# GLU stage of a streaming encoder on one Trainium2 core: operand stores moved to GpSimd's queue in two groups per tile, a third yT slot, meta frames split early, and state products later in the SSM

## The chip, the core and the metric

The kernel runs on one core of a Trainium2 chip, in one launch. The metric is the time of one execution on the device, in microseconds; the time of a kernel is the median of its runs. The core's engines each work through their own instructions in the order in which they were written: TensorE (PE, with PEld for its weight loads), VectorE (DVE), ScalarE (ACT), GpSimd (POOL) and SyncE (SP), which does nothing but issue DMAs here. DMAs can be issued from SP, from ACT and from POOL; each issue waits in its engine's queue for what it needs, and holds up whatever stands behind it.

## What is computed

One layer of a hybrid encoder on 2048 frames of 1024 numbers, with 16 learned meta frames ahead of them. Cut to what matters:

```python
hn = rms_norm(h, norm_mix)
u  = hn @ w_in                         # 64 groups of 16 channels
s_t = a * s_{t-1} + B u_t              # diagonal complex state, 64 per group
y  = gelu(Re(C s) + d_skip * u)
a, g = split(y @ w_glu)                # 1024 x 2048
h  = h + a * sigmoid(g)                # the GLU stage ends here
hn = rms_norm(h, norm_ffn)
b  = causal_dwconv(hn @ w_up)          # 1024 x 5632, three taps
b1, b2 = split(b)
out = h + (silu(b1) * b2) @ w_down     # 2816 x 1024
```

All of it is float32 in and out. Large products are taken as three float16 products of high and low halves (hi x hi, hi x lo, lo x hi).

## The kernel before

The program has three stages.

**The SSM stage.** The channels go in eight blocks of 128 (`cb`, 0 to 7). For each block, `emit_y` forms the outputs. Frames stand as 128 chunks of 16; for each pair of groups (`gp`, 0 to 3) a PSUM tile `yp` (tag `y`, two slots, which the small meta tile `mp` also uses) collects *direct* products, of the block's inputs `U` with a Toeplitz matrix (L588), and *carried* products, of the chunk states `Z` with `CA` (L590). ACT then takes the gelu of the whole tile (L592). `Toep` comes back from DRAM by eight DMAs, and right behind them on SP come the four DMAs that bring the states from `S` into `Z`. In this kernel direct and carried products alternate within one `gp`: one direct product of group 0, then its carried product, and so on. `mid`, when given, does a piece of the splitting of `w_glu` after each gelu.

**The GLU stage.** Sixteen tiles of 128 frames, `t` = 0 to 15 (`tile_of_step` gives the frames). For each tile: `load_y` brings `y` from DRAM (SP), `prep_y` splits it into `yT` (hi on ACT, L126; lo on DVE, L129; two slots), `glu_mm` does 96 matmuls of 512 columns on PE (L138) into four PSUM banks, alternately one of two sets of four, and `glu_post` does the rest: two sigmoids on ACT (L935), two products and two sums on DVE (L936, L937), the store of `h` (SP), the sum of squares on ACT (L940), the reciprocal root on POOL (L70, L72), the normalised tile `hn` on DVE (L943), and the splits into `hl` by `split2` (cast on ACT, L919; difference on DVE, L920). Odd tiles add and subtract halves of `hn` (L962, L963, L973, L974) and make three casts. SP then transposes `hl` into `hc` (L957) and stores part of it in `hd` (L982). The order of the instructions is written out by hand: what a function issues takes its place in each engine's queue at that point of the program.

Into this loop `keep_down` is woven. It is a generator that prepares the 77 operands of the down projection for the next stage: for each of 11 pairs of row blocks of `w_down` it loads two 512 KB pieces on POOL (`dst`, L874), makes seven operands, five of which are a sum or a difference formed on POOL (L889) and two of which are taken as they are, and for each operand casts the high half on ACT (L891), yields, takes the low half on DVE (L893), and stores the 256 KB result in DRAM one step late through `pend` (L896, SP). The results stand in four slots `wk`, one after the other (`NA = 4`). `keep(n)` takes n steps. Steps are taken at the head of the loop, between `prep_y` and `glu_post`, inside `glu_post` and behind it: six per tile.

The 16 meta frames pass the GLU in small products: `meta_load` brings `ytm` in after tile 3's load, `glu_meta` (at t = 3) splits it into `ym` (L995, L996) and issues 256 tiny matmuls (L1000, L1003) ahead of `glu_post(3)`, and `glu_meta2` (at t = 4) normalises.

**The FFN stage.** It streams the operands of the up and down projections through PE twice (`kb` = 0, 1). Its first weights are loaded by `w_load`, which is called at t = 14 behind `glu_post(14)`, and cast by `w_units` at t = 15 ahead of `glu_post(15)`.

Of the kernel before, what the change touches and what calls it, by code (L numbers as in the profile page):

```python
# [10 lines left out]
F16 = mybir.dt.float16  # L11
F32 = mybir.dt.float32
# [3 lines left out]
P = 128  # L16
D = 1024
DK = 8
# [26 lines left out]
def tile_kernel(ctx: ExitStack, tc: tile.TileContext, x, meta, norm_mix, norm_ffn, w_in, lam_re, lam_im, log_dt,  # L45
# [57 lines left out]
            A.copy(wg[0][:, dk, cs_], st)  # L103
            PO.tensor_tensor(wg[1][:, dk, cs_], st, wg[0][:, dk, cs_], op=ALU.subtract)

    yts = {}

    def tile_of_step(n):
        return n // 2 + 8 * (n % 2)
# [8 lines left out]
    def prep_y(t, d0=0, d1=DK, eng=A):  # L118

        w = P * (d1 - d0)  # L120
        if t not in yT:
            yT[t] = gl.tile([P, 2, DK, P], F16, tag="yT", bufs=2, name=f"yT_{t}")
        yt = yts.pop(t)
        hi, lo = (yT[t][:, i, d0:d1].rearrange("p b k -> p (b k)") for i in range(2))
        if eng is A:
            A.activation(hi, yt[:, 0:w], AF.Copy, scale=YS)  # L126
        else:
            V.tensor_scalar(hi, yt[:, 0:w], YS, None, op0=ALU.mult)
        V.scalar_tensor_tensor(lo, yt[:, 0:w], YS, hi, op0=ALU.mult, op1=ALU.subtract)  # L129
# [12 lines left out]
    with ExitStack() as c2:  # L142
# [424 lines left out]
        def emit_y(cb, mid=None):  # L567
            u, tp, ca, z = U[cb], Toep[cb], CA[cb], Z[cb]

            mp = psum.tile([P, 2], F32, tag="y", name=f"mp{cb}")  # L570
            for b in range(2):
                for f in range(2):
                    c0 = 224 if f == 0 else 96
                    for i in range(4):
                        g = 4 * b + i
                        PE.matmul(out=mp[32 * i:32 * i + 32, b:b + 1], lhsT=tp[:, g, c0:c0 + 32],
                                  rhs=u[:, 1 - f, g, 0:1], start=(f == 0), stop=(f == 1))
            mf = s5.tile([P, 2], F32, tag="mf", name=f"mf{cb}")
            A.activation(mf, mp, AF.Gelu_apprx_tanh)
            A.dma_start(out=ymd[:, :, cb], in_=mf)  # L580
            yf = s5.tile([P, 2, G, P], F32, tag="yf", name=f"yf{cb}")
            for gp in range(4):
                yp = psum.tile([P, 2, 2, P], F32, tag="y", name=f"yp{cb}_{gp}")
                for i in range(2):
                    g = 2 * gp + i
                    for r in range(2):
                        for f in range(r + 1):
                            PE.matmul(out=yp[:, r, i], lhsT=tp[:, g, P * (r - f):P * (r - f) + P],  # L588
                                      rhs=u[:, 1 - f, g, 1:P + 1], start=f == 0, stop=False)
                        PE.matmul(out=yp[:, r, i], lhsT=ca[:, g, 8 * r + 1:8 * r + 9].rearrange("p a b -> p (a b)"),  # L590
                                  rhs=z[:, g], start=False, stop=True)
                A.activation(yf[:, :, 2 * gp:2 * gp + 2], yp, AF.Gelu_apprx_tanh)  # L592
                if mid:
                    mid(gp)
            PO.dma_start(out=yd[cb].rearrange("r p g k -> p r g k"), in_=yf)

        def drive(*gens):
# [266 lines left out]
    def keep_down():  # L864

        lo_, hi_ = slice(0, 512), slice(512, 1024)
        st, n = {}, itertools.count()

        def load(j):
            if j < NH:  # L870
                for r in range(2):
                    st[j, r] = fw.tile([P, D], F32, tag="wst", bufs=NW, name=f"dst{j}_{r}")
                    f = j + NH * r
                    PO.dma_start(out=st[j, r], in_=w_down[0, f * P:(f + 1) * P])  # L874

        load(0)
        pend = None
        for j in range(NH):
            load(j + 1)
            s0, s1 = st.pop((j, 0)), st.pop((j, 1))  # L880
            b11, b12, b21, b22 = s0[:, lo_], s0[:, hi_], s1[:, lo_], s1[:, hi_]
            ta, tb = (fw.tile([P, 512], F32, tag="wtmp", bufs=1, name=f"dtmp{j}_{i}") for i in range(2))
            steps = [((1, j, 1), b11, None), ((0, j, 1), b22, None),
                     ((1, j, 0), ta, (b21, b11, ALU.subtract)), ((2, j, 0), b21, (b21, b22, ALU.add)),
                     ((0, j, 0), tb, (b12, b22, ALU.subtract)), ((2, j, 1), b22, (b11, b22, ALU.add)),
                     ((3, j, 0), b12, (b11, b12, ALU.add))]
            for (s, j_, i), src, sm in steps:
                if sm:
                    PO.tensor_tensor(src, sm[0], sm[1], op=sm[2])  # L889
                w = fw.tile([P, 2, 512], F16, tag=f"wc{next(n) % NA}", bufs=1, name=f"wk{s}_{j_}_{i}")  # L890
                A.activation(w[:, 0], src, AF.Copy, scale=GS)  # L891
                yield
                V.scalar_tensor_tensor(w[:, 1], src, GS, w[:, 0], op0=ALU.mult, op1=ALU.subtract)  # L893
                if pend:
                    pend()
                pend = (lambda w=w, k=kept["d", s, j_, i]: SY.dma_start(out=wcd[k], in_=w))  # L896
        pend()
        yield

# [6 lines left out]

    with ExitStack() as c3:
        gp = c3.enter_context(tc.tile_pool(name="gp", bufs=2, side="right"))
        x2 = {}

        def load_x2(t):
# [8 lines left out]
            V.tensor_tensor(dst[:, 1], src, dst[:, 0], op=ALU.subtract)  # L920

        kd_ = keep_down()

        def keep(n):
            for _ in range(n):
                next(kd_, None)

        def glu_post(t):
# [7 lines left out]
                V.scalar_tensor_tensor(sg[:, cs_], pt[o], 1.0 / (GS * YS), sg[:, cs_], op0=ALU.mult, op1=ALU.mult)  # L936
                V.tensor_tensor(h1[:, cs_], sg[:, cs_], h1[:, cs_], op=ALU.add)  # L937
            SY.dma_start(out=h1d[tile_of_step(t)], in_=h1)
            keep(1)
            A.activation(sg, h1, AF.Square, accum_out=ss)  # L940
            rs = rstd_of(gp, ss, P, f"b{t}")
            hn = hns[t] = gp.tile([P, D], F32, tag="hn", name=f"hn{t}")
            V.scalar_tensor_tensor(hn, h1, rs, gfr, op0=ALU.mult, op1=ALU.mult)  # L943
            keep(1)
            n = 20 if odd else 8
            hl = gp.tile([P, 2, n, P], F16, tag=f"hl{odd}", bufs=1, name=f"hl{t}")
            hf = hl.rearrange("p a n c -> p a (n c)")
# [11 lines left out]
            if odd:  # L959
# [3 lines left out]
                V.tensor_tensor(hn[:, lo_], hp[:, lo_], hn[:, lo_], op=ALU.subtract)  # L963
                split2(hf[:, :, 512:1536], hn)
                turn(12, 20)
                keep(1)
                if t == T - 1:
                    w_units(5)
                split2(hf[:, :, 0:512], sg[:, lo_])
# [7 lines left out]
            else:  # L977
                split2(hf, hn)
                turn(0, 8)
                keep(1)  # L980
            for i in range(2):
                SY.dma_start(out=hd[i][j, :, P * b0:P * (b0 + n)], in_=hf[64:128, i])  # L982

# [2 lines left out]
        def meta_load():  # L986
            for tt in range(2):
                SY.dma_start(out=ytm[:, tt], in_=ymd.rearrange("(i t h) b c -> t h b i c", t=2, h=16)[tt])
            SY.dma_start(out=xm, in_=meta[14:16].rearrange("t (c p) -> (t c) p", p=P))

        def glu_meta():

            ym = gp.tile([P, DK, 2, 2], F16, tag="ym", bufs=1, name="ym")
            ytr = ytm.rearrange("p t c -> p c t")
            A.activation(ym[:, :, 0], ytr, AF.Copy, scale=YS)  # L995
            V.scalar_tensor_tensor(ym[:, :, 1], ytr, YS, ym[:, :, 0], op0=ALU.mult, op1=ALU.subtract)  # L996
            pm = psum.tile([P, 16, 4], F32, tag="u", name="gm")
            for o in range(16):
                for dk in range(DK):
# [50 lines left out]
        prep_y(2)  # L1050
        load_y(3, gp_tile)
        meta_load()
        glu_post(0)
        for t in range(1, T):
            keep(1)
            if t + 1 < T:
                load_x2(t + 1)
            if t + 2 < T:
                prep_y(t + 2)
                if t + 3 < T:  # L1060
                    load_y(t + 3, gp_tile)
            keep(1)
            if t == 4:
                glu_meta2(*ms)
            if t == 3:
                ms = glu_meta()
            if t == T - 1:
                cl.close()
                ring[0] = fl = ctx.enter_context(tc.tile_pool(name="fl", bufs=2))
                w_units(3)  # L1070
                w_chain(0, 0)
            glu_post(t)
            keep(1)
            if t + 1 < T:
                glu_mm(t + 1)
            if t == T - 2:
# [316 lines left out]
```

## Time and profile before

| | us |
|---|---|
| median of 3 runs | 2102.34 |
| the runs | 2102.34, 2109.95, 2099.18 |
| the profiled execution's own time | 2114.33 |
| its span | 2112.5 |
| mean granted TensorE clock | 0.959 |
| PE busy | 1919.9 (91%) |
| DVE busy | 1531.7 (73%) |
| ACT busy | 643.3 (30%) |
| POOL busy | 707.0 (33%) |

All times in a profile count from the start of its span. The profiled execution took 12 us more than the median; its own time is 1.8 us more than its span. In a row of a timeline stand the start, the length, the engine, the line of the kernel, the operation, what it writes and reads, and in brackets how long the engine sat idle before it and what ended that. A matmul of 512 columns is shown with about 380 ns, though they start about 216 ns apart at the full clock, since they overlap. In the views of waits, each row has a total in us, a count, and the longest.

### The profile page before, as it was taken

The numbers are of one execution on the slowest core, as the hardware profiler recorded it, in microseconds if no ns is written. First come the engines' busy times: TensorE is split into PE (matmuls) and PEld (weight loads), VectorE is DVE, ScalarE is ACT, GpSimd is POOL, SyncE is SP. The second block draws the span as 40 slices with busy tenths as digits, with TensorE's granted clock in tenths as the row PEclk, the third lists the DMA queues.
The fourth block names the chain that finished last, engine by engine and source line by source line (L and its number), as shares of the span: only waits on it lengthen the run. The fifth ranks groups of instructions, "written<-read, shape, count | busy, mean of one in ns | idle before, by whom it ended". The sixth has DMA issues, their size and how long they took to land.

```text
span 2112.5 us, 29565 instructions
## 1 busy us (share of the span) xinstructions
PE 1919.9 (91%) x11116; PEld 965.2 (46%) x11116; DVE 1531.7 (73%) x2084; ACT 643.3 (30%) x1083; POOL 707.0 (33%) x749
## 2 busy tenths in 40 slices
PE   3797999679599888899999999899999999999999
PEld 3455665644344333344444444344444444444444
DVE  4489988955556555699999999895266666668882
ACT  4432322403323323354444443111022223232110
POOL 4221211413233332454556666661000001216730
PEclk9898999889799999999999999999999999999999
DMA  9957557884476666744543436954533333336443
GB/s 197 194 113 147 123 129 143 191 218 132 143 194 204 176 192 162 218 144 151 162 153 130 150 130 178 205 151 119 155 100 104 101 102 103 100 104 156 130 123 96
DMA packets 315626, 312.90 MB, mean 148 GB/s; under 512 B 116556, under 2 KB 220188, under 8 KB 315484
## 3 DMA queue, kind: packets, MB, share of 16 engines
q1 hardware_dynamic: 294396, 257.43, 46.5%
q0 software_dynamic: 11664, 38.84, 6.7%
q10 hardware_dynamic: 9424, 14.76, 2.8%
q8 instruction: 87, 1.43, 0.3%
q14 instruction: 55, 0.45, 0.1%
HBM read 180.93 MB, written 102.69 MB: 134 GB/s over the span
## 4 chain that ended last, share of the span: by engine, by line
PE 52%; DVE 18%; DMA 11%; issue 7%; ACT 4%; SPq 3%; POOL 2%; DVEq 0%; ACTq 0%; POOLq 0%
PE p L76 10%; PE p L78 10%; PE p L77 10%; PE po L76 5%; PE po L77 5%; PE po L78 5%; DMA wcd<-wk 4%; DMA fst<-in_ffn_w_up_dram 2%; PE g L138 1%; DMA Z<-S 1%; PE yp L588 1%; DVE wk L893 1%; DMA hnT<-hl 1%; PE yp L590 1%; DVE x L937 1%
## 5 line engine op out<-in xcount | busy, mean ns | idle before, releaser
L76 PE MATMUL p<-hc,wc 128*128 128x512 f16 x1232 | 468.8, 380 | 6.9 <-ACT wc L852 3.6
L78 PE MATMUL p<-hc,wc 128*128 128x512 f16 x1232 | 469.0, 381 | 6.5 <-DVE wc L858 6.3
L77 PE MATMUL p<-hc,wc 128*128 128x512 f16 x1232 | 468.6, 380 | 0.9 <-DMA hc<-hl 0.9
L138 PE MATMUL g<-wg,yT 128*128 128x512 f16 x1536 | 344.7, 387 | 27.7 <-DVE sg L936 27.7
L138 PEld LDWEIGHTS <-yT 128*128 128x128 f16 x1536 | 152.5, 99 | 218.0 <-issue 45.0
L76 PE MATMUL po<-wc,act 128*128 128x512 f16 x616 | 236.8, 384 | 12.1 <-DVE res L1343 8.3
L77 PE MATMUL po<-wc,act 128*128 128x512 f16 x616 | 236.6, 384 | 0.0
L78 PE MATMUL po<-wc,act 128*128 128x512 f16 x616 | 236.5, 384 | 0.0
L78 PEld LDWEIGHTS <-wc 128*128 128x128 f16 x1232 | 120.8, 98 | 156.1 <-DVE wc L858 8.9
L76 PEld LDWEIGHTS <-wc 128*128 128x128 f16 x1232 | 120.7, 98 | 145.6 <-issue 5.4
L77 PEld LDWEIGHTS <-wc 128*128 128x128 f16 x1232 | 120.8, 98 | 138.9 <-issue 2.5
L858 DVE SCALAR_TENSOR_TENSOR wc<-fst,wc 128x512 f16<-128x512 f32 x132 | 126.1, 959 | 23.1 <-ACT t8b L1184 11.1
L76 PE MATMUL u<-hnT,win 128*128 128x512 f16 (+2 forms) x352 | 114.1, 335 | 31.4 <-DMA hnT<-hl 29.0
L1239 ACT CAST act<-hc 128x512 f16<-128x512 f32 x88 | 54.1, 618 | 255.3 <-DVE hc L1238 149.5
L77 PE MATMUL u<-hnT,win 128*128 128x512 f16 (+2 forms) x352 | 113.9, 334 | 9.4 <-DMA hnT<-hl 9.4
L852 ACT ACTIVATE wc<-fst 128x512 f16<-128x512 f32 x132 | 79.4, 625 | 128.6 <-POOL fst L832 118.8
L1236 POOL TENSOR_TENSOR hc<-act 128x512 f32<-128x512 f16 x66 | 93.0, 1415 | 75.4 <-DVE hc L1238 75.4
L1343 DVE SCALAR_TENSOR_TENSOR res<-po,res 128x512 f32<-128x512 f32 x96 | 60.7, 682 | 77.1 <-PE po L78 76.3
L1191 POOL COPY hu<-halo 128x2 f32<-128x2 f32 x44 | 12.1, 283 | 311.5 <-DVE act L1124 191.1
L78 PE MATMUL u<-hnT,win 128*128 128x512 f16 (+2 forms) x352 | 113.9, 334 | 0.0
L1115 ACT ACTIVATE act<-hu,cwt 128x1024 f32<-128x1024 f32 x44 | 54.6, 1241 | 182.3 <-DVE hu L1207 133.4
L1240 DVE TENSOR_TENSOR act<-hc,act 128x512 f16<-128x512 f32 x88 | 95.4, 1104 | 16.8 <-ACT act L1239 14.1
(370 smaller groups left out, 3249.5 us busy)
## 6 DMA issues: line engine op xcount, KB each, us to landing
wc<-wcd SPq DMA_DIRECT2D x308, 256.0 KB, 2.7
wcd<-wc SPq DMA_DIRECT2D x154, 256.0 KB, 2.0
fst<-in_ffn_w_up_dram SPq DMA_DIRECT2D x44, 512.0 KB, 5.4
wcd<-wk SPq DMA_DIRECT2D x77, 256.0 KB, 3.4
dst<-in_ffn_w_down_dram POOLq DMA_DIRECT2D x22, 512.0 KB, 5.4
ud<-us SPq DMA_DIRECT2D x32, 258.0 KB, 4.6
U<-ud SPq DMA_DIRECT2D x16, 516.0 KB, 6.1
Toep<-kd SPq DMA_DIRECT2D x64, 128.0 KB, 5.5
```

What stands on the lines that cost most here:

```text
L76: PE.matmul(out=ps, lhsT=sh, rhs=mh, start=first, stop=False)
L77: PE.matmul(out=ps, lhsT=sh, rhs=ml, start=False, stop=False)
L78: PE.matmul(out=ps, lhsT=sl, rhs=mh, start=False, stop=last)
L138: PE.matmul(out=gps[t][o], lhsT=yT[t][:, a, dk], rhs=wg[b][:, dk, 512 * o:512 * o + 512], start=(dk == 0 and a + b == 0), stop=(dk == DK - ...
L588: PE.matmul(out=yp[:, r, i], lhsT=tp[:, g, P * (r - f):P * (r - f) + P], rhs=u[:, 1 - f, g, 1:P + 1], start=f == 0, stop=False)
L852: A.activation(w[:, 0], src, AF.Copy, scale=GS)
L858: V.scalar_tensor_tensor(w[:, 1], src, GS, w[:, 0], op0=ALU.mult, op1=ALU.subtract)
L1115: A.activation(y, hu[:, 2:18], AF.Identity, bias=cwt[:, 3, c:c + 1], scale=cwt[:, 2, c:c + 1])
L1236: PO.tensor_tensor(t_, act16[:, fa_, ra, 1], act16[:, fb, rb, 1], op=op)
L1239: A.copy(act16[:, fd, rd, 0], s_)
L1240: mix_los.append(lambda: V.tensor_tensor(act16[:, fd, rd, 1], s_, act16[:, fd, rd, 0], op=ALU.subtract))
L1343: V.scalar_tensor_tensor(h, po[t4, i], sign / (GS * AS), h, op0=ALU.mult, op1=ALU.add)
```

## The change

In the SSM's `emit_y`, the products of a `gp` are taken apart into `direct(gp)` and `carried(gp)`, and the direct products of the next `gp` are issued ahead of the carried products of this one. Only the first product of a PSUM tile carries the start flag. In the GLU stage, `yT` gets three slots (the third in another pool), all tiles' tags changed accordingly. `keep_down` gets a yield behind its first load, and that first step is taken before the loop; its stores are issued by POOL instead of SP; its steps are taken in two groups of three, at the head of the loop and behind `glu_post`, and none inside `glu_post`. The split of the meta frames moves from `glu_meta` into `meta_prep`, called right behind `meta_load`.

```diff
-    yts = {}
+    yts, yt_pools = {}, [gl, gl]
...
-            yT[t] = gl.tile([P, 2, DK, P], F16, tag="yT", bufs=2, name=f"yT_{t}")
+            yT[t] = yt_pools[t % 3].tile([P, 2, DK, P], F16, tag=f"yT{t % 3}", bufs=1, name=f"yT_{t}")
...
-            for gp in range(4):
-                yp = psum.tile([P, 2, 2, P], F32, tag="y", name=f"yp{cb}_{gp}")
+            yps = {}
+
+            def direct(gp):
+                yp = yps[gp] = psum.tile([P, 2, 2, P], F32, tag="y", name=f"yp{cb}_{gp}")
                 for i in range(2):
                     g = 2 * gp + i
                     for r in range(2):
                         for f in range(r + 1):
                             PE.matmul(out=yp[:, r, i], lhsT=tp[:, g, P * (r - f):P * (r - f) + P],
-                                      rhs=u[:, 1 - f, g, 1:P + 1], start=f == 0, stop=False)
+                                      rhs=u[:, 1 - f, g, 1:P + 1], start=i + r + f == 0, stop=False)
+
+            def carried(gp):
+                yp = yps.pop(gp)
+                for i in range(2):
+                    g = 2 * gp + i
+                    for r in range(2):
                         PE.matmul(out=yp[:, r, i], lhsT=ca[:, g, 8 * r + 1:8 * r + 9].rearrange("p a b -> p (a b)"),
-                                  rhs=z[:, g], start=False, stop=True)
+                                  rhs=z[:, g], start=False, stop=i + r == 2)
                 A.activation(yf[:, :, 2 * gp:2 * gp + 2], yp, AF.Gelu_apprx_tanh)
                 if mid:
                     mid(gp)
+
+            direct(0)
+            for gp in range(4):
+                if gp < 3:
+                    direct(gp + 1)
+                carried(gp)
...
         load(0)
+        yield
         pend = None
...
-                pend = (lambda w=w, k=kept["d", s, j_, i]: SY.dma_start(out=wcd[k], in_=w))
+                pend = (lambda w=w, k=kept["d", s, j_, i]: PO.dma_start(out=wcd[k], in_=w))
...
+        yt_pools.append(gp)
...
         kd_ = keep_down()
+        next(kd_)
...
             SY.dma_start(out=h1d[tile_of_step(t)], in_=h1)
-            keep(1)
             A.activation(sg, h1, AF.Square, accum_out=ss)
             rs = rstd_of(gp, ss, P, f"b{t}")
             hn = hns[t] = gp.tile([P, D], F32, tag="hn", name=f"hn{t}")
             V.scalar_tensor_tensor(hn, h1, rs, gfr, op0=ALU.mult, op1=ALU.mult)
-            keep(1)
...
                 turn(12, 20)
-                keep(1)
...
                 turn(0, 8)
-                keep(1)
...
-        def glu_meta():
+        def meta_prep():
 
             ym = gp.tile([P, DK, 2, 2], F16, tag="ym", bufs=1, name="ym")
...
+            return ym
+
+        def glu_meta(ym):
...
         meta_load()
+        ym = meta_prep()
         glu_post(0)
         for t in range(1, T):
-            keep(1)
+            keep(3)
...
-            keep(1)
             if t == 4:
                 glu_meta2(*ms)
             if t == 3:
-                ms = glu_meta()
+                ms = glu_meta(ym)
...
             glu_post(t)
-            keep(1)
+            keep(3)
```

## The prediction

> **What bounds the kernel now.** I read the page first (shares of the engines, the granted clock over the span), then the span cut at the stages' borders, then in the GLU stage who waits for whom, and last the instructions of each engine in order of time.
>
> ```profile
> span 2112.5 us, 29565 instructions
> PE 1919.9 (91%) x11116; PEld 965.2 (46%) x11116; DVE 1531.7 (73%) x2084; ACT 643.3 (30%) x1083; POOL 707.0 (33%) x749
> PEclk9898999889799999999999999999999999999999
> ...
> 160.00:452.00 292.00, 238.40 (x2152) 173.70 (x2151) 257.25 (x518) 83.16 (x157) 61.33 (x83) 0.89 0.73 151
> 484.00:855.00 371.00, 312.62 (x1615) 141.93 (x1613) 211.01 (x235) 118.89 (x187) 113.46 (x118) 0.92 0.64 178
> 855.00:2112.50 1257.50, 1229.27 (x6247) 562.59 (x6246) 960.23 (x1086) 374.12 (x623) 471.95 (x454) 0.99 0.47 135
> ```
>
> Columns of the last three: stretch, its length, busy time (count) of PE, PEld, DVE, ACT and POOL, granted clock, DMA share, GB/s. PE holds 91% of the whole, but the stage that changes is not PE's: from 484 to 855 us it is busy 313 of 371 us, at a clock of 0.92, and no other engine is fuller. The FFN behind it is PE's and keeps its length; what the change is worth lies ahead of 855 us. The waits from 484 to 851:
>
> ```profile
> ACT wk L891 <- DMA wcd<-wk: 114.1, 19, 15.1
> PE g L138 <- DVE sg L936: 27.7, 11, 7.6
> PE gm L1000 <- DVE ym L996: 23.9, 1, 23.9
> ...
> L896 SPq DMA_DIRECT2D wcd<-wk x77: 319/609/9194, 497.8 to 827.1; - x77
> DMA to landing us min/median/max: 2.0/3.4/15.0
> ```
>
> ACT stands 114 us before a cast of a kept operand, because the store that frees its slot has not landed, though a store lands in 3.4 us once issued. PE's 27.7 us are a consequence: it waits for banks that `glu_post` has yet to read. Why the stores come late is seen in tile 7, an odd one:
>
> ```profile
> 687.86 4.46 SPq L957 DMA_TRANSPOSE hc<-hl  x2
> 692.37 2.26 SPq L982 DMA_DIRECT2D hd<-hl  x2
> 694.67 1.09 SPq L896 DMA_DIRECT2D wcd<-wk  x1
> ...
> 699.90 0.63 ACT L891 ACTIVATE wk<-dtmp 128x512 f16<-128x512 f32 x1 [10.06 <-DMA wcd<-wk]
> ```
>
> The store stands on SP behind transposes that wait for the tile's last cast; it goes out at 694.67, lands near 699.8, and ACT, which has the next sigmoid right behind that cast, sat 10.06 us. So the stage is a chain through ACT's queue, and its measure is the start of each tile's first sigmoid, S(t):
>
> ```profile
> 485.92 1.08 ACT L935 ACTIVATE sg<-g 128x512 f32<-128x512 f32 x2
> ...
> 600.78 1.07 ACT L935 ACTIVATE sg<-g 128x512 f32<-128x512 f32 x2
> ...
> 805.63 1.07 ACT L935 ACTIVATE sg<-g 128x512 f32<-128x512 f32 x2
> 822.59 1.06 ACT L935 ACTIVATE sg<-g 128x512 f32<-128x512 f32 x2
> 836.33 1.08 ACT L935 ACTIVATE sg<-g 128x512 f32<-128x512 f32 x2
> ```
>
> These are S(0), S(4), S(12), S(13) and S(14): 114.9 us for the first four tiles, 204.9 for the next eight (51.2 a pair), 30.7 for the last two. PE needs 96 x 0.216 = 20.7 us for a tile, 41.5 a pair, so it is not the bound. Behind S(14) the loads of the FFN's first weights follow at a fixed distance, so the FFN starts as S(14) does.
>
> **The change, part by part.** *A tile's own work, without steps in it.* From tile 8 (S = 700.43) and tile 13 (S = 822.59, whose steps were nearly over):
>
> ```profile
> 705.93 2.28 DVE L943 SCALAR_TENSOR_TENSOR hn<-x,rsb,gfr 128x1024 f32<-128x1024 f32 x1 [1.54 <-POOL rsb L72]
> 709.32 1.22 DVE L920 TENSOR_TENSOR hl<-hn,hl 128x1024 f16<-128x1024 f32 x1 [0.51 <-ACT hl L919]
> 705.87 1.25 POOL L889 TENSOR_TENSOR dst<-dst 128x512 f32<-128x512 f32 x1
> ...
> 828.27 1.28 DVE L943 SCALAR_TENSOR_TENSOR hn<-x,rsb,gfr 128x1024 f32<-128x1024 f32 x1 [1.55 <-POOL rsb L72]
> 836.46 1.23 DVE L920 TENSOR_TENSOR hl<-hn,hl 128x1024 f16<-128x1024 f32 x1 [1.11 <-ACT hl L919]
> ```
>
> An even tile's last DVE instruction ends 710.5 - 700.4 = 10.1 us behind its S, an odd one's 837.7 - 822.6 = 15.1, or 16.1 with `hn` at 2.28 instead of 1.28 us. Those 2.28 us show the second thing to count: `hn` began 0.06 us behind a POOL sum of 1.25 us and was held for most of it. DVE and POOL shut each other out; a step's DVE half is 0.68 us alone and about 1.75 beside a POOL sum.
>
> The Trainium skill, "SBUF — State Buffer", section "Who interferes with whom", states this as a rule: a VectorE instruction with two SBUF inputs and a GpSimd instruction that reads SBUF exclude each other. The trace agrees (2.28 against 1.28). It goes on that DMAs issued from GpSimd starve beside VectorE's two-port modes, and advises the hardware queues. I see no such mode in this loop's steady work, so the sum by it is the same.
>
> *The steps, in two groups, stores on POOL.* SP loses 77 issues x 0.61 = 47 us, which costs nothing and gains only order: `h1d`, transposes, `hd` and `yt` no longer have stores among them. POOL gains 77 issues. No 256 KB store from POOL is in the trace; the nearest rows:
>
> ```profile
> yd<-yf POOLq DMA_DIRECT2D x8, 1024.0 KB, 4.5
> dst<-in_ffn_w_down_dram POOLq DMA_DIRECT2D x22, 512.0 KB, 5.4
> wcd<-wc SPq DMA_DIRECT2D x154, 256.0 KB, 2.0
> ...
> L874 POOL DMA_DIRECT2D dst<-in_ffn_w_down_dram x22: 527/536/625, 460.0 to 766.4; - x22
> ```
>
> Issue: 0.55 us. Landing: from 2.0 (same size, from SP, in the FFN) to 5.4 (twice the size, a load on POOL); I take SP's own 3.4, nearest in size, direction and stage. On POOL a step is a store (0.55) and, in five of seven, a sum (1.27): 1.85 us. Queued behind a store that waits: the next sum, `x2`'s load, and this tile's reciprocal root, so now the tile's own chain passes POOL. The store of step k needs DVE's half of k, which needs ACT's half, which needs the sum of k; with DVE held by the next sum every second step takes 2.5 instead of 1.85, a mean of 2.2. Then an even tile, all steps with sums: DVE free at 10.1, half of the waiting step 10.8, store and sum 12.6, four more steps at 2.2 give 21.4, the cast 0.63 and `prep_y` 1.04 give S(t+1) at 23.0. Six steps hold 4.3 sums, not 6, and 1.7 loads of 0.55. A step without a sum is not free: a cast needs the store of four steps back, issued two steps back, so two steps take at least 0.55 + 3.4 = 4.0 us. Laying the seven-step cycle against the groups position by position, an even tile comes to 20.9 to 23.5; I take 21.8, and for an odd one 6.0 more, 27.8. That is 49.6 a pair against 51.2. The waits for SP go, and what is late next is the string store, sum, cast, half; the steps also lose the cover they had inside `glu_post`.
>
> *Third yT slot, early ym.* `prep_y(2)` need not wait for `glu_mm(0)`: PE ends tile 0 after 144 of the 156 matmuls of
>
> ```profile
> 452.27 33.83 PE L138 MATMUL g<-wg,yT 128*128 128x512 f16 x156
> 483.55 1.06 ACT L126 ACTIVATE yT<-yt 128x1024 f16<-128x1024 f32 x1 [22.87 <-PE g L138]
> 553.47 0.20 ACT L995 ACTIVATE ym<-ytm 128x16 f16<-128x16 f32 x1
> 561.54 1.06 ACT L935 ACTIVATE sg<-g 128x512 f32<-128x512 f32 x2
> 586.93 0.17 DVE L1023 MEMSET one<- 128x128 f32 x1
> 589.85 0.17 DVE L1030 TENSOR_TENSOR hm<-hm,gains 128x16 f32<-128x16 f32 x1
> ```
>
> at 452.27 + 144 x 0.216 = 483.4, so S(0) is there instead of at 485.92: 2.5 gained. `ym` is now split long before PE wants it, so PE's 23.9 us at tile 3 go, and with them the 7 us that ACT stood for the tiny products (553.5 to 561.5). Of this only ACT's part counts, as PE is not the bound. What stays is about 1 us at t = 3 and 3 us (586.9 to 590.0) at t = 4. S(0) to S(1) has one group: even tile to the last cast 8, three steps 4.5, `prep_y` 1: 13.5. The early `load(0)` costs two POOL issues, 1.1 us, while POOL waits for DVE anyway: nothing; without that cover, 1.1.
>
> *The sum in the GLU stage.* S(0) to S(4): 13.5 + 27.8 + 21.8 + 27.8 + 4 = 94.9, against 114.9: 20.0 gained. S(4) to S(12): 4 x 49.6 = 198.4, against 204.9: 6.5 gained. S(12) to S(14): 21.8, then tile 13 with its last two operands and no `prep_y`: 16.1 + 0.7 + 0.55 + 1.27 + 0.63 = 19.3; together 41.1 against 30.7: 10.4 lost, since three steps were taken in tile 0 before and now stand behind tile 13. With S(0): 2.5 + 20.0 + 6.5 - 10.4 = 18.6 gained.
>
> *The SSM's products.* From block 1 of `emit_y`, and the waits for the states:
>
> ```profile
> PE yp L590 <- DMA Z<-S: 18.9, 8, 10.1
> 207.67 0.77 PE L590 MATMUL yp<-Z,CA 128*128 128x128 f32 x2 [1.01 <-DMA Z<-S]
> 214.63 0.39 PE L590 MATMUL yp<-Z,CA 128*128 128x128 f32 x2
> 217.29 0.60 ACT L592 ACTIVATE yf<-yp 128x512 f32<-128x512 f32 x1 [1.64 <-PE yp L590]
> 219.52 0.60 ACT L592 ACTIVATE yf<-yp 128x512 f32<-128x512 f32 x1 [1.64 <-PE yp L590]
> ```
>
> A `gp` is ten products in 2.23 us, 0.223 each. One direct product stood ahead of the wait, now twelve: 11 x 0.223 = 2.45 us that can fill it. But the wait is (18.9 - 10.1) / 7 = 1.26 us in seven blocks and long only in the last: filled 7 x 1.26 + 2.45 = 11.3. Against that stands a new wait: `direct(2)` takes the slot of `yp0` right behind `carried(0)`, so PE stands for the gelu (0.60 and about 0.25 to hand over), and again at `direct(3)`: 2 x 0.85 x 8 = 13.6. Net 2.3 lost. Bounds: 13.6 lost if the fill brings nothing; for the gain, the half clock: from 207.67 to 219.5 the block took 11.9 us instead of 8.7 for its 39 products left, so 3.2 went to the cold clock; if half of it goes by starting 2 us earlier, 8 x 1.6 less 2.3, 10 gained. I take 2.3 lost, as row by row nothing warms the clock for sure.
>
> **Sum:** 18.6 - 2.3 = 16.3 us off 2114.33, 2098.0, or 0.9923 of it. The profiled run lies 12 us above the median, and I carry the ratio: 0.9923 x 2102.34 = 2086.
>
> **The rivals.** *It goes further* (15%): the groups run without the lock-outs, at 1.85 a step; 6 x 0.35 = 2.1 a tile over 11 tiles takes 23 more, but not all steps have sums, so some 14: 2072. For it: 0.68 is the half's usual length (its median). Against: `hn` at 2.28 in most tiles.
>
> *Nothing comes of it* (22%): the steady pairs take 51 to 53 instead of 49.6 and the end takes its 10: near 2100. The Trainium skill, "DMA: Bandwidth & Descriptors", section "Issuing engines are not separate DMA queues", says that another issuing engine saves only the issuer's time; by that the store's move is worth nothing. The row above (10.06 us behind SP's transposes) speaks against it: what is waited for is order on SP.
>
> *Slower* (13%): POOL's stores share one queue with its 512 KB loads (`x2`, and two `dst` per seven steps), and the group's third cast meets a store that lands behind them. Hidden up to about 5.6 us of landing; at 5.4 plus a second load ahead of it, 8, each group waits 1.5 more, 3 a tile, 33 over 11 tiles: 16.3 gained turn into 17 lost, 2119. It decides from 1.5 us a tile.
>
> **How the numbers follow.** My forecast has 50%, its own range 2076 to 2096. 0.5%, 10.5 us, is about what a measurement of this kernel can tell from no change. Faster by more: most of my case (42 of 50) and the first rival, 57%. Within: 8 of mine and the second rival, 30%. Slower: 13%. For eight in ten I go from a little below the first rival, 2066, to between the second and the third, 2110.
>
> **What would show it.** SP's stores gone from its timeline and no ACT wait of 10 us behind `wcd`; ACT's waits for stores well under 114 us, and in their place waits for POOL's sums; S(t) differences near 22 and 28 us alternately; `gm` without a wait of 24 us; S(14) near 818; PE waits at `direct(2)` and `direct(3)` of 0.8 us, 16 of them. Wrong if even and odd tiles fall to PE's 20.7, if stores from POOL land in 6 us or more, or if the SSM ends over 5 us earlier or later.

## The result: 1% slower

The changed kernel takes 2125.4 us (median of four, 2119.8 to 2128.6) against 2101.2 for the kernel before, run beside it: 1.0104 of it, 95% interval 1.0068 to 1.0140. The forecast was 16 us faster. The profiled execution took 2126.13 us; its span is 11.8 us longer than the one of before, half of what the medians show, because the part ahead of the SSM's blocks, which the change doesn't touch, happened to take 8 us less in it. So the stages are compared each from its own start.

The page of after has:

```profile
span 2124.3 us, 29587 instructions
PE 1920.0 (90%) x11116; PEld 966.0 (45%) x11116; DVE 1527.3 (72%) x2084; ACT 645.0 (30%) x1083; POOL 733.3 (35%) x826
```

And its stretches that answer to the three shown of before (stretch, length, busy time of PE, PEld, DVE, ACT and POOL, granted clock, DMA share, GB/s):

```profile
171.00:457.00 286.00, 230.74 (x2048) 164.79 (x2047) 245.58 (x493) 80.29 (x153) 61.47 (x83) 0.90 0.70 147
487.00:867.00 380.00, 314.38 (x1619) 142.62 (x1618) 207.07 (x233) 117.96 (x184) 141.69 (x197) 0.91 0.62 176
867.00:2124.00 1257.00, 1228.72 (x6248) 562.60 (x6248) 959.88 (x1086) 374.42 (x623) 471.54 (x454) 0.99 0.47 135
```

The work is the same, PE's within 0.1 us. POOL has 28 us more in the GLU stage: its stores take 43.6 us there, its sums 70 instead of 84. The FFN is as long as before, the GLU stage 9 us longer. The SSM's blocks, from the last gelu of the first to that of the last, take 285.1 us (171.55 to 456.67) instead of 272.5. The waits of after in the GLU stage, and the landing of the stores from section 6 of the page; below them two waits of POOL in the kernel before, from 484 to 851 us:

```profile
POOL wcd L911 <- DVE wk L908: 103.7, 30, 10.1
...
ACT wk L906 <- DMA wcd<-wk: 42.7, 15, 7.7
...
ACT wk L906 <- POOL dst L904: 41.7, 22, 3.5
...
ACT wk L906 <- POOL dtmp L904: 40.4, 14, 4.1
...
PE gm L1016 <- DVE sg L953: 2.1, 1, 2.1
```

```profile
wcd<-wk POOLq DMA_DIRECT2D x77, 256.0 KB, 5.2
```

```profile
POOL dst L874 <- DVE wk L893: 52.2, 13, 11.9
...
POOL dtmp L889 <- DVE wk L893: 27.3, 8, 6.9
```

ACT's wait for stores fell from 114 to 43 us and PE's 23.9 us at `gm` to 2.1, as forecast. In their place ACT waits 82 us for POOL's sums (29.8 before), and POOL stands 104 us at stores that wait for DVE. POOL stood for DVE's halves before too, 79.5 us at loads and sums whose buffers a half had yet to read; what is new is that the stores stand there, for longer, with the sums behind them. Tiles 8 and 9 in order of time show how these hang together:

```profile
702.46 1.06 ACT L952 ACTIVATE sg<-g 128x512 f32<-128x512 f32 x2
...
712.66 1.23 DVE L936 TENSOR_TENSOR hl<-hn,hl 128x1024 f16<-128x1024 f32 x1 [1.11 <-ACT hl L935]
...
723.50 0.63 ACT L906 ACTIVATE wk<-dst 128x512 f16<-128x512 f32 x1 [0.46 <-DMA wcd<-wk]
...
724.98 1.06 ACT L952 ACTIVATE sg<-g 128x512 f32<-128x512 f32 x2
...
731.05 0.62 POOL L911 DMA_DIRECT2D wcd<-wk  x1
731.12 2.95 DVE L959 SCALAR_TENSOR_TENSOR hn<-x,rsb,gfr 128x1024 f32<-128x1024 f32 x1 [2.14 <-POOL rsb L72]
731.70 1.28 POOL L904 TENSOR_TENSOR dtmp<-dst,dst 128x512 f32<-128x512 f32 x1
...
742.11 0.68 DVE L908 SCALAR_TENSOR_TENSOR wk<-dst,wk 128x512 f16<-128x512 f32 x1
...
743.09 0.58 POOL L911 DMA_DIRECT2D wcd<-wk  x1 [10.12 <-DVE wk L908]
743.69 1.27 POOL L904 TENSOR_TENSOR dst<-dst 128x512 f32<-128x512 f32 x1
...
745.00 0.63 ACT L906 ACTIVATE wk<-dst 128x512 f16<-128x512 f32 x1 [3.53 <-POOL dst L904]
...
754.54 0.63 ACT L906 ACTIVATE wk<-dst 128x512 f16<-128x512 f32 x1 [2.63 <-DMA wcd<-wk]
...
756.02 1.06 ACT L952 ACTIVATE sg<-g 128x512 f32<-128x512 f32 x2
```

`keep_down` yields between a step's cast on ACT and its half on DVE. The last cast ahead of tile 9's sigmoid runs at 723.50; its half is queued on DVE behind the whole `glu_post` of tile 9 and runs at 742.11. POOL issues one store and one sum from 731.05 on, and then stands 10.12 us at the store of that half. The next sum is behind it in POOL's queue and starts at 743.69, when the tile's own chain is over. From there the steps run one behind the other, sum, cast, half, until 756.02. The group's third cast waits another 2.63 us for a store that went out in the same group.

### The profile page after: what moved, and what is told of

The parts are those of the page before. It is cut to its first block, busy times and chain, and to the rows that moved or that the text cites. A ratio compares the mean times of both kernels' runs of the same rounds, so it can differ in the third digit from the quotient of the medians.

```text
span 2124.3 us, 29587 instructions
## 1 busy us (share of the span) xinstructions
PE 1920.0 (90%) x11116; PEld 966.0 (45%) x11116; DVE 1527.3 (72%) x2084; ACT 645.0 (30%) x1083; POOL 733.3 (35%) x826
## 4 chain that ended last, share of the span: by engine, by line
PE 57%; DVE 13%; DMA 11%; issue 7%; ACT 5%; POOL 4%; SPq 2%; ACTq 0%; DVEq 0%; POOLq 0%
PE p L78 10%; PE p L76 10%; PE p L77 10%; PE po L76 5%; PE po L77 5%; PE po L78 5%; DMA wcd<-wk 3%; PE yp L590 3%; PE g L138 2%; DMA hnT<-hl 2%; DMA Z<-S 1%; DVE hn L959 1%; DMA Toep<-kd 1%; PE yp L598 1%; DVE wk L908 1%
## 5 line engine op out<-in xcount | busy, mean ns | idle before, releaser
L76 PE MATMUL po<-wc,act 128*128 128x512 f16 x616 | 235.6, 383 | 13.1 <-DVE res L1359 10.2
L872 DVE SCALAR_TENSOR_TENSOR wc<-fst,wc 128x512 f16<-128x512 f32 x132 | 126.0, 958 | 22.3 <-ACT wc L866 12.5
L76 PE MATMUL u<-hnT,win 128*128 128x512 f16 (+2 forms) x352 | 113.2, 332 | 24.2 <-DMA hnT<-hl 13.9
L77 PE MATMUL u<-hnT,win 128*128 128x512 f16 (+2 forms) x352 | 113.1, 332 | 14.7 <-DMA hnT<-hl 14.7
```

Of the source, the lines that this page charges most:

```text
L76: PE.matmul(out=ps, lhsT=sh, rhs=mh, start=first, stop=False)
L77: PE.matmul(out=ps, lhsT=sh, rhs=ml, start=False, stop=False)
```

## The experiments

Each kernel was timed beside the kernel before, in five rounds; the figure is the ratio to it with its 95% interval. "Slot and ym" is the third yT slot with the early ym. In the GLU stage the measure is S(t), the start of the first sigmoid of tile t.

**1. The SSM's order alone.** Kernel before with `direct` and `carried` as in the change, nothing else.

> Kernel before with the new order of the SSM's products alone; GLU stage as before. Theory A (the SSM order loses: two waits for a gelu per block, 0.95 us each in the trace of after, against a fill worth little): last gelu of block 1 to last gelu of block 8 about 285 us against 272.5, the total 10 to 12 us above before. Theory B (the SSM is worth nothing in either direction, the GLU's steps lose it all): within 3 us of before. My prediction's own term would be 2.3 us lost.

1.0034 (1.0017 to 1.0050), 7 us slower. PE's waits in the SSM, from the chain of who waits for whom:

```profile
PE yp L590 <- ACT yf L600: 11.0, 16, 0.7
...
PE yp L598 <- DMA Z<-S: 10.3, 2, 9.4
```

Before, PE waited 18.9 us for the states in eight blocks; now 10.3 in two. In exchange it waits 16 times for a gelu. The blocks take 279.3 us in this profile, against 272.5 before. The SSM's part of the loss is real, somewhat smaller than the 10 to 12 us that Theory A read from one pair of profiles.

**2. A fill that takes no bank.**

```
direct(0)
direct(1)
carried(0)
carried(1)
for gp in range(2, 4):
    direct(gp)
    carried(gp)
```

> Kernel before with the SSM's products as direct(0), direct(1), carried(0), carried(1), direct(2), carried(2), direct(3), carried(3): eight direct products still stand ahead of the wait for the states (one before, twelve by the change's order), but nothing that takes a bank stands ahead of carried(1). Theory A (what costs is the wait for the gelu behind carried(0) and carried(1), the fill itself gains): no PE wait at the direct products above 0.3 us, 3 to 8 us under before. Rival (the fill brings nothing, because the states come later for another reason, or because a cold clock follows the wait whatever fills it): within 3 us of before. Second rival (it is the two start flags or the bank shared by both that cost, not the order): 8 us or more above before.

0.9964 (0.9949 to 0.9978), 7.6 us faster; Theory A holds. The first row is from the timeline of the changed kernel, which has experiment 1's order, the second from that of this one; both are `direct(2)` of the second block. The third is this kernel's longest PE wait in its products:

```profile
205.49 1.60 PE L590 MATMUL yp<-U,Toep 128*128 128x128 f32 x12 [0.69 <-ACT yf L600]
```

```profile
200.50 1.56 PE L590 MATMUL yp<-U,Toep 128*128 128x128 f32 x12
```

```profile
PE yp L598 <- DMA Z<-S: 8.8, 1, 8.8
```

The fill was right; `direct(gp + 1)` ahead of `carried(gp)` spoils it, since with two `yp` slots it asks for the slot that the gelu is just reading. The expectation miscounts: `direct(0)` and `direct(1)` are six products each (x12 in a row, since each shows twice), so twelve stand ahead of the wait here as in the change, and only the places of `direct(2)` and `direct(3)` differ. The twelve take the wait away in all blocks but the last. Single profiles scatter, but the orders stay apart in all of them: the blocks take 266.5 to 273.3 us in the ten profiles with the order of before, 279.3 and 285.1 with the change's, and 262.8 to 266.4 in the five with this one.

**3. All of the GLU part**, SSM as before.

> Kernel before with all of the change's GLU part (groups of steps, stores from POOL, third yT slot, early ym, early load), the SSM's products as before. Theory A (the loss is split between the SSM, about 11, and the GLU, about 10): S(0) to S(14) about 363 us against 350.4, the total 8 to 12 us above before. Theory B (the SSM loses all of it): within 3 us. Prediction: 18.6 us faster.

1.0060 (1.0038 to 1.0082), 12.6 us slower in the medians' ratio; S(0) to S(14) takes 363.9 us against 350.4. With experiment 1 the parts add to 1.0094, the whole measured 1.0104. So both parts lose, the GLU part perhaps more (the intervals overlap), and what follows takes the GLU part to pieces.

**4. Slot and ym alone**, six steps spread over each tile and stores from SP, as before.

> Kernel before with the third yT slot and the early ym alone; seven steps spread over each tile as before, stores from SP. Theory A (these two gain, the groups give it back): the 23.9 us wait at gm gone, S(0) 2.5 earlier, S(0) to S(4) about 103 us against 114.9, S(4) to S(14) as before at 235.5: 10 to 17 us faster. Rival (PE's wait at gm was covered, since ACT's chain and not PE sets the stage): only the 2.5 of S(0) and up to 3 us, total 2 to 5 us faster.

0.9952 (0.9937 to 0.9967), 10 us faster. S(0) to S(4) is 103.4 us against 114.9, S(4) to S(14) 237.4 against 235.6. This part of the change does what the prediction said of it.

**5. Stores from POOL, steps still spread.** Experiment 4 with one edit:

```
- pend = (... SY.dma_start(out=wcd[k], in_=w))
+ pend = (... PO.dma_start(out=wcd[k], in_=w))
```

> The kernel with third slot and early ym (10 us faster than before by itself), with the 77 stores of kept operands moved from SP to POOL, and the seven steps a tile spread as before. Theory P (the stores are what costs: they land later from POOL, 5.2 us against 3.4, and POOL stands for DVE at each of them, so sums come late): 15 us or more lost against the kernel with slot and ym alone, 5 or more above before. Theory G (the grouping costs, because three steps in a row have nothing between them that covers the string sum, cast, half): at least as fast as with slot and ym alone, 10 us or more under before, ACT's waits for stores well under 111 us because SP's transposes are no longer ahead of them.

0.9795 (0.9773 to 0.9816), 42 us under before, 33 of them (0.9952 less 0.9795) from this word. ACT's wait for stores in experiment 4, then its waits for sums and stores in this one, and below them the steady tiles S(4) to S(12) of experiment 3 and of this one:

```profile
ACT wk L891 <- DMA wcd<-wk: 111.0, 18, 15.8
```

```profile
ACT wk L891 <- POOL dst L889: 60.7, 25, 3.7
ACT wk L891 <- POOL dtmp L889: 42.4, 16, 4.3
...
ACT wk L891 <- DMA wcd<-wk: 7.2, 3, 3.2
```

```profile
575.20:795.80 220.60, 195.35 (x861) 86.01 (x859) 116.11 (x128) 68.06 (x106) 87.16 (x120) 0.93 0.63 176
```

```profile
560.80:741.90 181.10, 181.10 (x841) 82.12 (x840) 126.06 (x128) 67.25 (x106) 85.94 (x117) 1.00 0.75 219
```

111 us became 7, though the stores land in 4.4 us instead of 3.4 at the median: what was waited for was order on SP. A pair of tiles takes 45.3 us, PE has no gap left in these tiles (its ends are modelled) and its granted clock is 1.00 instead of 0.93. Theory P fell: the store's move is the best of the change, and the grouping must have eaten it. One thing warns against reading the waits as the loss: ACT waits 103 us for sums here, more than the 82 of the change, in a kernel that is far faster. A wait costs by what stands behind it, and its total alone does not tell.

**6. Groups with stores from SP:** experiment 3 with that word put back.

> All of the change's GLU part with one edit: the 77 stores back on SP. Groups, shift of three steps, third slot, early ym as in the change; the SSM as before. It was 12.6 us above before with the stores on POOL. Theory P (POOL's stores cost): 10 us or more under that, about the time before. Theory G (grouping costs): within 5 us of it, or worse, since the stores stand behind hd and the transposes on SP; ACT's waits for sums (84 us in 36 waits) stay above 50 us.

1.0048 (1.0029 to 1.0067), not to be told from experiment 3. ACT's wait for stores is 98.2 us again, that for sums 22.7 instead of 84. In groups with this cut the queue makes no difference: by the totals, order on SP costs what the hold of POOL costs. POOL is not free here either: it stands 68.6 us at sums and 63.0 us at loads for halves that have yet to read their buffers. Theory G's figure for the sums missed, its total held.

**7. The same without the lag of a step** (stores from SP, each issued right behind its half).

> As the kernel with groups and stores on SP, with one more edit: each store is issued right behind its own half on DVE, not behind the half of the next step. In a group of three the third cast needs the slot of four steps back, whose store was issued only at the start of the same group; without the lag it was issued in the group before. Theory L (what costs in a group is this landing, 41 us of ACT in 14 waits): these waits fall under 10 us and the kernel gains 8 us or more against groups with stores on SP. Theory G (the string sum, cast, half and the lost cover): less than 4 us gained.

1.0010 (0.9995 to 1.0024), 8 us better than experiment 6 by the ratios and 6 by the medians, but the waits for stores stayed at 93.3 us in 16, with a landing of 6.0 us at the median. It lies between the two theories and settles nothing; an earlier issue on SP still stands behind the transposes.

**8. Seven steps a tile in groups** instead of six: the second `keep(3)` of a tile becomes `keep(4)`, otherwise experiment 3.

> All of the change's GLU part, SSM as before, with one edit: the second group of a tile has four steps instead of three, so that the kept operands are done in tile 11 as before and not in tile 13. Theory E (the steps that now stand behind tile 13 cost 10 us, a term of my sum): S(12) to S(14) 31 instead of 42 and S(4) to S(12) hardly longer: 8 us or more faster than the groups of three. Theory G (a step in a group costs 2 us or more wherever it stands): S(4) to S(12) longer by 8 x 2, so within 6 us of the groups of three.

1.0022 (1.0008 to 1.0037), 8 us less than the groups of three by the ratios, which is Theory E's bound, with 3 to 13 us left open by the two intervals. S(12) to S(14) fell from 41.9 to 26.6, but S(0) to S(4) rose from 101.4 to 111.0 and S(4) to S(12) from 220.6 to 224.9. In the profiles S(0) to S(14) is nearly the same (362.5 and 363.9): 15.3 us saved at the end, 13.9 paid elsewhere. Neither theory's figures hold (Theory G wanted 16 more in S(4) to S(12), it was 4.3). The expectation is wrong in one thing: the kernel before also takes six steps a tile and has its last casts in tile 12, so this kernel, which is done in tile 11, is not a return to it. Its steps were moved from behind tile 13 into the other tiles and cost nearly as much there; the place behind tile 13 is at most a small part of the loss.

**9. Two steps moved out of `glu_post`.** Experiment 5 with the steps behind `h1d`'s store and behind `hn` taken out and put behind the tile (`keep(3)` at its end), the third inner one left.

> The spread kernel with stores from POOL (2055 us, 42 under before), with the two steps behind h1d's store and behind hn taken out of glu_post and put behind it, seven a tile still. Theory G (what is lost is the cover that a tile's own chain gave to the steps): 2 of the 3 inner steps moved, so about half or more of the 50 us between spread and grouped come back as a loss: 2075 to 2095. Rival (only the step count a tile, the early load or the place of the prep counts): within 8 us of 2055.

0.9967 (0.9952 to 0.9981): 36 us of the gain of experiment 5 go with two steps that changed their place, their number and all else left alone. S(4) to S(12) goes from 181.0 to 204.2. That it is the grouping is shown, for a step that is cut between cast and half.

**10. The cut behind the half.** Experiment 3 with the yield put later:

```
  A.activation(w[:, 0], src, AF.Copy, scale=GS)
- yield
  V.scalar_tensor_tensor(w[:, 1], src, GS, w[:, 0], ...)
  if pend:
      pend()
  pend = (...)
+ yield
```

> All of the change's GLU part, SSM as before, with one edit: a step ends behind its half on DVE and the store of the step before, not between cast and half. With the change's cut the last half of a group is queued on DVE behind the next tile's whole glu_post, and the group's first store stands on POOL for it (30 waits, 103 us, the longest 10.1), with the sums of the next group behind it. Theory H (this hold of POOL is what costs: POOL stands idle through glu_post and the string of sums starts only behind it): POOL's waits for a half fall under 40 us, ACT's waits for sums fall from 84 to under 45 us, pairs from 55 to about 48, and the kernel is 20 us or more faster than the same with the change's cut (2110), so 2090 or less. Theory G (the grouping itself costs, whatever stands on POOL): less than 8 us.

0.9898 (0.9877 to 0.9919), 34 us faster than the same groups with the change's cut (1.0060). S(4) to S(12) is 198.5 instead of 220.6. But the figures for the waits missed: POOL still waits 87.4 us for halves in 28 waits (of 103.4), and ACT's waits for sums fell from 84 to 66 us, not to 45. Tile 8 shows what changed:

```profile
665.97 1.06 ACT L937 ACTIVATE sg<-g 128x512 f32<-128x512 f32 x2
...
672.06 1.25 POOL L890 TENSOR_TENSOR dst<-dst 128x512 f32<-128x512 f32 x1
...
673.27 0.63 POOL L896 DMA_DIRECT2D wcd<-wk  x1
673.93 1.60 POOL L890 TENSOR_TENSOR dtmp<-dst,dst 128x512 f32<-128x512 f32 x1
...
675.38 0.63 ACT L892 ACTIVATE wk<-dst 128x512 f16<-128x512 f32 x1
...
675.92 0.61 ACT L892 ACTIVATE wk<-dtmp 128x512 f16<-128x512 f32 x1
...
677.63 0.57 POOL L896 DMA_DIRECT2D wcd<-wk  x1 [2.10 <-DVE wk L893]
...
686.25 1.06 ACT L937 ACTIVATE sg<-g 128x512 f32<-128x512 f32 x2
```

The hold stays, but the store ahead of it has its half already, so two sums get through while the tile's chain runs, and two casts follow back to back. The second effect: each store goes out one step earlier, and ACT's wait for landings falls from 41 to 22 us. So Theory H holds in the total and only half in its mechanism: one sum more ahead of the hold, and an earlier store, 18 and 19 us less of ACT's waits.

**11. The later cut, with stores from SP.**

> Groups of three with the later cut (a step ends behind its half), stores on SP. The same with stores on POOL was 0.9898 of before, with the change's cut and SP 1.0048. Theory Q (two separate costs: the hold of POOL by a store that waits, which SP's stores don't have, and the order on SP behind transposes; the later cut also sends two stores out one group earlier): 1.000 or above, so POOL's queue is worth 1% in groups too. Rival (the cut is what counts and the queue doesn't): 0.988 to 0.993.

1.0010 (0.9990 to 1.0030), in the total as Theory Q said: without the old cut the queue is worth 1.1% in groups too. The two costs mask each other: the later cut alone, on SP, brings 8 us (1.0048 to 1.0010), the queue alone, with the old cut, nothing (1.0060), both together 31 (0.9898).

**12. What gained, together:** experiments 2 and 4.

> What gained, together: the SSM's order direct(0), direct(1), carried(0), carried(1), direct(2), carried(2), direct(3), carried(3), the third yT slot and the early ym; steps, stores and the rest as before. The two lie in different stages: if they add, 7.6 and 10.0 give 17 to 18 us under before, 0.9916. Rival (one hides the other, as both move work behind the same weight loads): 10 to 12 under.

0.9913 (0.9892 to 0.9935). They add.

**13. Experiments 2 and 5 together.**

> Stores from POOL with the steps spread over the tile, third slot, early ym, and the SSM's order with eight direct products ahead of the wait. If the gains add: 0.9795 x 0.9964 = 0.976 of before, about 2047 us. If the SSM's gain is lost behind the stages it feeds: 2055.

0.9765 (0.9741 to 0.9788), 2048.6 us. They add again.

**14. The same with the later cut.**

> The best kernel so far (spread steps, stores from POOL, slot, early ym, the SSM's filled order; 0.9765) with the later cut. Theory H (the hold is long only where a whole tile lies between cast and half): spread, POOL's waits for a half are 29 us, the longest 2.2, so at most 10 us gained, more likely within 4. Rival (the cut costs by itself, as the half then follows its cast with nothing between): 5 us or more slower.

0.9678 (0.9650 to 0.9705), 2034.4 us: 18 us more, where both theories allowed 10 at most. POOL's time at its stores, and ACT's waits for sums, in experiment 13 and then here:

```profile
POOL wcd L912 <- issue: 55.7, 17, 4.2
ACT wk L907 <- POOL dst L905: 55.1, 23, 3.7
ACT wk L907 <- POOL dtmp L905: 44.4, 18, 4.3
...
POOL wcd L912 <- DVE wk L909: 29.3, 17, 2.2
```

```profile
POOL wcd L911 <- DVE wk L908: 72.2, 39, 4.5
ACT wk L907 <- POOL dst L905: 34.4, 19, 2.8
...
ACT wk L907 <- POOL dtmp L905: 22.7, 11, 3.0
```

I had counted only the 29.3 us that name DVE, not the 55.7 us of the same stores called "issue"; of those 17 waits, 15 end 0.5 us behind the end of a half on DVE, so those are the same hold. ACT's waits for sums fall by 42 us; a pair takes 42.2 us, 0.7 above PE's 41.5. So the later cut gains with the steps spread as well, about half of what it gains in groups. And with the later cut in both, groups are still 29.6 us behind in S(4) to S(12): 198.5 in experiment 10 against 168.9 here.

**15. With the early load of the change too.**

> As the best kernel with the later cut, and the first two 512 KB loads of w_down issued ahead of the stage, as the change has it. S(0) to S(1) was 16.7 in the spread kernel and 13.4 in groups: if the early load is the reason, up to 3 us faster; if it was the count of steps in tile 0, the same within 2 us.

0.9664 (0.9630 to 0.9697), 2031.4 us. S(0) to S(1) is the same 16.4: the early load isn't what made it short in groups, and 1.4 per thousand under the last is within the intervals. This is the fastest version, 3.4% under before and 4.4% under the changed kernel (0.9664 / 1.0104), though not to be told from experiment 14.

The GLU versions side by side (S differences in us, from the rows of the first sigmoids):

| slot and ym in all but the first | S(0)-S(4) | S(4)-S(12) | S(12)-S(14) | ratio |
|---|---|---|---|---|
| before (spread, SP) | 114.9 | 204.9 | 30.7 | 1 |
| spread, SP (4) | 103.4 | 206.7 | 30.7 | 0.9952 |
| spread, POOL (5) | 90.1 | 181.0 | 35.5 | 0.9795 |
| two moved, POOL (9) | 102.8 | 204.2 | 36.7 | 0.9967 |
| groups, POOL (3) | 101.4 | 220.6 | 41.9 | 1.0060 |
| groups, SP (6) | 99.5 | 219.9 | 38.6 | 1.0048 |
| groups, later cut, POOL (10) | 93.5 | 198.5 | 37.2 | 0.9898 |
| groups, later cut, SP (11) | 99.2 | 214.4 | 37.9 | 1.0010 |
| spread, later cut, POOL, SSM filled (14) | 85.6 | 168.9 | 35.8 | 0.9678 |

## Why the prediction was wrong

**Point by point**, gains positive, as forecast and as the two profiles have it:

| term | forecast | measured |
|---|---|---|
| S(0) behind the SSM | 2.5 | 2.6 |
| S(0) to S(4) | 20.0 | 14.2 (114.9 to 100.7) |
| S(4) to S(12) | 6.5 | -15.1 (204.9 to 220.0) |
| S(12) to S(14) | -10.4 | -11.2 (30.7 to 41.9) |
| SSM's blocks | -2.3 | -12.6; alone, timed, -7 |

**The step that failed most** is the length of a steady pair: 49.6 us forecast, 55.0 measured, 21.6 us over four pairs. It fails in three sizes. Two lie in a tile's own work, put at 10.1 and 16.1 us; tiles 8 and 9 took 11.4 (702.46 to 713.9) and 17.2 us (724.98 to 742.2), 2.4 a pair more. `hn` takes 2.95 us, not 2.28, because a store issue of 0.62 us now stands ahead of the sum on POOL and the sum lies later in `hn`; and `prep_y`'s 1.23 us on DVE now stand directly ahead of the first product of the tile. Third, the landing: I took 3.4 us, it is 5.2, and ACT waits 42.7 us for it, 36.8 of them in these eight tiles. That is more than the 12 us that own work leaves of the 21.6, since the forecast already had 4.0 us for two steps without sums; what share of the miss the landing has can't be told apart further. Up to there the nearest rival, stores that land late behind loads, was the right direction. That its price of 2119 was near is partly luck, since it has neither the longer own work nor more than 2.3 us of loss in the SSM.

**What lay under it** is a wrong comparison. I had the order right ("half of the waiting step", then store, then sum, behind the tile's chain) but held it for the groups' given length and asked only whether it beat 51.2. I put the gain of the store's move at the order on SP, rightly, and never priced that move with the steps left in place: there it is worth 33 us (experiment 5). The grouping, with the shift and the early load that came with it, costs 2.65% on top of that (0.9795 to 1.0060). The later cut takes 1.6% off the groups (experiment 10), but 0.9% off the spread steps too (experiment 14). As an estimate, spread steps with the later cut and the SSM as before would stand at 0.9795 x 0.9678 / 0.9765 = 0.9708, and groups at 0.9898 are 1.9% above that. So only some 0.8% of what the grouping costs goes with the change's cut, and the larger part goes with the grouping whichever cut is used. "The steps also lose the cover they had inside `glu_post`" stood in the prediction as one clause with no price; two steps moved cost 36 us (experiment 9). By what path the lost cover costs that much no run took apart. With the later cut the groups take 198.5 us for S(4) to S(12) and 93.5 for S(0) to S(4), near the 198.4 and 94.9 that I forecast for the change, but that is luck: the forecast had the second sum held behind the half, as it is in the change and not with the later cut.

**The Trainium skill's rule**, in "DMA: Bandwidth & Descriptors", section "Issuing engines are not separate DMA queues", that another issuing engine saves only the issuer's time: I set it aside for the row of 10.06 us behind SP's transposes. With the steps spread the trace bears that out (111 us of waits to 7, 33 us of time); it is the issuer's time that counts here, as order and not as 0.6 us an issue. In groups with the change's cut the move is worth nothing (1.0060 against 1.0048), as the rule would have it, though for another reason.

**The SSM term** had the right two sides and the right sign. The new waits are 16 as forecast, 11.0 us in all where I had 13.6. The fill was put at 11.3, and that was too high: the order that fills without the waits gains 7.6 us, the order of the change loses 7, and PE's waits for the states fell by 8.6 us in experiment 1. Of the 14.7 us between the two orders PE's waits show 12.5 (21.3 in experiment 1, 8.8 in experiment 2); the rest lies within the intervals. The 12.6 us of the table come from one pair of profiles, and the profile of before is among the longer ones of its order.

**The end** came out as forecast, 41.9 us against 41.1. But it was no loss of the kind I took it for: with the steps put ahead of tile 12 most of it is paid there (experiment 8).

**Held as said:** SP without stores, no wait of 24 us at `gm`, 16 waits at `direct(2)` and `direct(3)`, three-step S(0) to S(1) of 13.4 us against 13.5. S(14), forecast near 818, came at 850.2.

## What to carry to other kernels

A DMA issue that waits for its data holds its whole engine: before moving one to a compute engine's queue, list what is queued behind it there, and put the producer's instruction in the same piece of work, not behind a yield (worth 34 us in groups and 18 us spread here). Changes that belong together are to be priced one by one and in pairs; here one word gained 33 us and a regrouping made for it took back 55. An order that fills a wait with more work must not ask for a buffer that the next consumer still reads.

## What the runs showed of the hardware

- A queue in order: POOL stood 10.12 us at one DMA issue with a sum of 1.27 us behind it whose inputs were there.
- DVE's `hn` (1.28 us alone) takes 2.28 us when a POOL sum of 1.25 us begins with it, and 2.94 us when the sum begins 0.57 us into it: about 1.1 us are left after the sum's end either way, so the late sum costs more.
- The same 256 KB stores land in 3.4 us at the median spread on SP, 4.4 spread on POOL, 5.2 in groups on POOL, 4.4 in groups on SP, 6.0 there without the lag, and 5.4 spread on POOL with the later cut. Neither the queue nor the grouping alone orders these.
- PE's granted clock in the steady tiles went from 0.93 (PE busy 195 of 221 us) to 1.00 (no gap), in experiments 3 and 5; what the higher clock was worth by itself no run took apart.
